# Rotary embedding on one core: when cosine is asked for, and how the last batch leaves

## The chip, the core and the metric

The kernel runs on one core of a Trainium2 chip. Its engines work side by side, each through its own list of instructions in order: VectorE (DVE) does the arithmetic, ScalarE (ACT) converts number formats, and GpSimd (POOL), SyncE (SP) and ACT issue DMA transfers. Tensors lie in the device memory; the engines work on the on-chip memory of 128 partitions. All transfers are carried by the same 16 DMA engines, fed from three queues: q0, the software queue, with what POOL issues; q1 with what SP issues; q10 with what ACT issues. [...] TensorE is not used.

The metric is device time in microseconds (us), the median over runs. Lower is better.

## The reference

`x` is float32 of shape (8, 2048, 16, 64): batch, position, head, head dimension. `cos` and `sin` are float32 of shape (2048, 32).

```python
x1 = x[..., :head_dim // 2]
x2 = x[..., head_dim // 2:]
out1 = x1 * cos - x2 * sin      # cos, sin broadcast over batch and head
out2 = x1 * sin + x2 * cos
return np.concatenate([out1, out2], axis=-1).astype(np.float32)
```

It reads 67 MB and writes 67 MB, with three vector operations for each element.

## The kernel before

**Tiling.** Each of the 128 partitions holds 16 neighbouring positions, called rows here (J = 16; a row is H x D = 1024 numbers, 4 KB in float32). A batch is 16 rows per partition. `buf` has five float16 slots of one batch each; batch b lies in slot b mod 5.

**Tables.** `sin_f` and `cos_f` come in as float32 by SP (line 50) and ACT (line 51). ACT makes float16 copies: `sin_h` with the negated sine in its first half (lines 101 and 102), `cos_h` (line 103).

**Rotation.** `rotate(b, j0, j1)` has three DVE operations: `v` = swapped halves times `sin_h` (line 87), `x` times `cos_h` in place (line 91), and their sum in place (line 93).

**The software queue.** All of POOL's transfers go through `queue` (line 57), which keeps them in program order. Loads and stores of whole batches and pairs of batches go there: load rows 2 to 15 of batch 0; store row 0 of batch 0; load batches 1 and 2; load 3 and 4; store rows 1 to 15 of batch 0; store 1 and 2; load 5; load 6 and 7; store 3 and 4; store 5 and 6; and the last rows of batch 7. POOL waits at each for what it needs, so a transfer is issued only when the one before it has been issued.

**The start.** The first two rows of batch 0 do not go through the software queue. ACT asks for them, as float32, into `head`, which is a view of the still unused last slot (line 52). ACT then narrows them to float16 into slot 0 in two steps, `narrow_head(0, 1)` and `narrow_head(1, 2)` (line 96). In ACT's order this stands behind the cosine copy of line 103. After the first step DVE rotates row 0, POOL stores it, and behind that store POOL issues the loads of batches 1 to 4.

**The end.** Batch 7 leaves in three pieces: rows 0 to 8 and rows 9 to 13 as two software stores, and rows 14 and 15 as float32: ACT widens them into `tail`, a view of slot 3 (line 127), and SP stores them (line 128). A dependency added by hand (`gate`) holds SP's store back until the store of rows 0 to 8 has landed.

Of the kernel before, what the change touches and what calls it, by code (L numbers as in the profile page):

```python
# [1 line left out]

# [4 lines left out]


@with_exitstack  # L10
def kernel(
    ctx: ExitStack,
    tc: tile.TileContext,
    x: bass.AP,
    cos: bass.AP,
    sin: bass.AP,
    out: bass.AP,
):
    nc = tc.nc
    f16 = mybir.dt.float16  # L20
    f32 = mybir.dt.float32

    B, S, H, D = x.shape
    Dh = D // 2
    P = nc.NUM_PARTITIONS
    J = S // P
    SLOTS = 5
    JA = 2
    JE = 2
    JF = 1  # L30

    pool = ctx.enter_context(tc.tile_pool(name="rope", bufs=1))
    buf = pool.tile([P, SLOTS, J, H, D], f16)
    v = pool.tile([P, J, H, D], f16)
    sin_f = pool.tile([P, J, Dh], f32)
    cos_f = pool.tile([P, J, Dh], f32)
    cos_h = pool.tile([P, J, Dh], f16)
    sin_h = pool.tile([P, J, D], f16)

    def words(slot, rows):  # L40
        flat = buf[:, slot, 0 : 2 * rows].rearrange("p j h d -> p (j h d)")
        return flat.bitcast(f32)

    head = words(SLOTS - 1, JA)
    tail = words(SLOTS - 2, JE)
    rows_in = x.rearrange("b (p j) h d -> p b (j h d)", j=J)
    rows_out = out.rearrange("b (p j) h d -> p b (j h d)", j=J)
    W = H * D

    nc.sync.dma_start(out=sin_f, in_=sin.rearrange("(p j) d -> p j d", j=J))  # L50
    nc.scalar.dma_start(out=cos_f, in_=cos.rearrange("(p j) d -> p j d", j=J))  # L51
    nc.scalar.dma_start(out=head, in_=rows_in[:, 0, 0 : JA * W])

    ring = []

    def queue(dst, src):
        dma = nc.gpsimd.dma_start(out=dst, in_=src)  # L57
        if ring:
            tc.add_manual_dep(
                dma.ins,  # L60
                ring[-1].ins.name,
                mybir.DependencyInfo(mybir.DependencyClass.NoSync, mybir.DependencyReason.DATA),
                reason="order of the ring",
            )
        ring.append(dma)
        return dma

    def part(b, n, j0, j1):
        s = b % SLOTS
        return buf[:, s : s + n, j0:j1].rearrange("p n j h d -> p n (j h d)")  # L70

    def load(b, n=1, j0=0):
        return queue(part(b, n, j0, J), rows_in[:, b : b + n, j0 * W : J * W])

    def store(b, n=1, j0=0, j1=J):
        return queue(rows_out[:, b : b + n, j0 * W : j1 * W], part(b, n, j0, j1))

    def rotate(b, j0=0, j1=J):
        n = j1 - j0
        js = slice(j0, j1)  # L80
        xt = buf[:, b % SLOTS, js]
        vt = v[:, js]
        shape = [P, n, H, 2, Dh]
        sin_b = sin_h[:, js, :].rearrange("p j (e d) -> p j e d", e=2).unsqueeze(2).to_broadcast(shape)
        cos_b = cos_h[:, js, :].unsqueeze(2).to_broadcast([P, n, 2 * H, Dh])
        xe = xt.rearrange("p j h (e d) -> p j h e d", e=2)
        nc.vector.tensor_mul(  # L87
            out=vt.rearrange("p j h (e d) -> p j h e d", e=2), in0=xe[:, :, :, ::-1, :], in1=sin_b
        )
        xw = xt.rearrange("p j h (e d) -> p j (h e) d", d=Dh)  # L90
        nc.vector.tensor_mul(out=xw, in0=xw, in1=cos_b)  # L91
        xa = xt.rearrange("p j h d -> p (j h d)")
        nc.vector.tensor_add(out=xa, in0=xa, in1=vt.rearrange("p j h d -> p (j h d)"))  # L93

    def narrow_head(j0, j1):
        nc.scalar.copy(  # L96
            out=buf[:, 0, j0:j1].rearrange("p j h d -> p (j h d)"), in_=head[:, j0 * W : j1 * W]
        )

    load(0, j0=JA)  # L100
    nc.scalar.copy(out=sin_h[:, :, Dh:D], in_=sin_f)  # L101
    nc.scalar.mul(out=sin_h[:, :, 0:Dh], in_=sin_f, mul=-1.0)  # L102
    nc.scalar.copy(out=cos_h, in_=cos_f)  # L103
    narrow_head(0, JF)
    narrow_head(JF, JA)
    rotate(0, 0, JF)
    store(0, j1=JF)
    load(1, 2)
    load(3, 2)
    rotate(0, JF, J)  # L110
    store(0, j0=JF)
    rotate(1)
    rotate(2)
    store(1, 2)
    load(5)
    load(6, 2)
    rotate(3)
    rotate(4)
    store(3, 2)
    rotate(5)  # L120
    rotate(6)
    store(5, 2)
    rotate(7)
    gate = store(7, j1=9)
    store(7, j0=9, j1=J - JE)

    nc.scalar.copy(out=tail, in_=buf[:, (B - 1) % SLOTS, J - JE : J].rearrange("p j h d -> p (j h d)"))  # L127
    end = nc.sync.dma_start(out=rows_out[:, B - 1, (J - JE) * W : J * W], in_=tail)
    tc.add_manual_dep(
        end.ins,  # L130
        gate.ins.name,
        mybir.DependencyInfo(mybir.DependencyClass.Sync, mybir.DependencyReason.DATA),
        reason="the last rows go out behind this part",
    )


# [1 line left out]
_INS = ['x', 'cos', 'sin']  # L138
_OUTS = [((8, 2048, 16, 64), 'float32')]


# [23 lines left out]
```

## Time and profile before

| What | Value |
| --- | --- |
| median of 3 runs | 316.48 us (316.36 to 316.49) |
| the profiled execution's own time | 316.32 us |
| its span | 314.6 us |
| DVE busy | 209.1 us, 66% |
| ACT busy | 6.8 us, 2% |
| POOL busy | 7.9 us, 3% |
| moved by DMA | 101.71 MB; 67.63 MB read from and 67.11 MB written to the device memory |
| one DVE operation on a batch | 8.69 us, 7 times in each of three lines |
| store of rows 0 to 8 of batch 7 | 4608 KB, 35.5 us from issue to landing |
| store of rows 9 to 13 of batch 7 | 2560 KB, 41.0 us |
| SP's store of rows 14 and 15 | 1024 KB, issued at 305.26, 8.4 us |
| the transfers of ACT and SP at the start | head 1024 KB, 12.1 us; cosine 256 KB, 3.9 us; sine 256 KB, 3.7 us |

The span is the profiled part of an execution; 1.72 us of the execution's own time lie around it. Sizes of loads are those of the data that arrive, so a software load that converts to float16 counts half of what it reads. In the rows of the profile "a<-b" names what is written and read, an engine name with q (ACTq, SPq) is that engine's sequencer issuing a transfer, and the part in brackets tells how long the engine had been idle and what ended the wait. In lists of stretches each line has the stretch, its length, busy time and number of instructions of DVE, ACT and POOL, the TensorE clock (of no meaning here), the mean share of the 16 DMA engines and GB/s. A packet is counted in the stretch in which it ends, so a share can be over 1.

### The profile page before, as it was taken

The page shows a single profiled execution, that of the slowest core. Times are in us where ns is not written, and L with a number is a line of the kernel's source. Part 1 is how long each engine was busy: PE and PEld are TensorE (multiplying, and loading weights), DVE is VectorE, ACT ScalarE, POOL GpSimd, SP SyncE. Part 2 cuts the span into 40 slices and gives each one's busy share as a digit, 9 for nine tenths or more (in the row PEclk, how much of TensorE's full clock was granted, in tenths as well). Part 3 has the DMA queues.
Part 4 walks back from the last instruction along what each step waited for, and adds up shares of the span by engine and source line. Part 5 has one row for each costly group of instructions (what it writes and reads, how often), then busy time and mean ns, then how long its engine had stood idle before and what let it go on. Part 6 is the DMA issues. An engine that isn't in the chain of part 4 may idle for free.

```text
span 314.6 us, 113 instructions
## 1 busy us (share of the span) xinstructions
DVE 209.1 (66%) x27; ACT 6.8 (2%) x7; POOL 7.9 (3%) x16
## 2 busy tenths in 40 slices
DVE  0109991089999999999994399903999999200000
ACT  3200000000000000000000000000000000200000
POOL 1020000000000000000000000000000000100000
DMA  7989999999999899999999999999999999999998
GB/s 230 261 193 249 267 200 200 200 267 200 200 200 325 375 500 400 400 400 533 400 200 221 246 200 200 250 217 333 400 517 417 400 400 525 408 400 400 433 425 342
DMA packets 3072, 101.71 MB, mean 323 GB/s; under 512 B 256, under 2 KB 256, under 8 KB 640
## 3 DMA queue, kind: packets, MB, share of 16 engines
q0 software_dynamic: 2496, 99.09, 98.1%
q1 hardware_dynamic: 288, 1.31, 1.2%
q10 hardware_dynamic: 288, 1.31, 1.0%
HBM read 67.63 MB, written 67.11 MB: 428 GB/s over the span
## 4 chain that ended last, share of the span: by engine, by line
DVE 59%; DMA 19%; another core or an unknown queue 7%; ACT 1%; issue 0%; POOL 0%; ACTq 0%; DVEq 0%
DVE v L87 20%; DVE buf L91 20%; DVE buf L93 20%; DMA buf<-in_x_dram 19%; ACT buf L127 1%; ACT buf L96 0%; POOL out_dram L57 0%; ACTq L51 0%; DVEq L87 0%
## 5 line engine op out<-in xcount | busy, mean ns | idle before, releaser
L87 DVE TENSOR_TENSOR v<-buf,sin_h 128x16384 f16<-128x16384 f16 (+2 forms) x9 | 69.7, 7744 | 59.7 <-DMA buf<-in_x_dram 45.3
L91 DVE TENSOR_TENSOR buf<-buf,cos_h 128x16384 f16<-128x16384 f16 (+2 forms) x9 | 69.7, 7744 | 0.3
L93 DVE TENSOR_TENSOR buf<-buf,v 128x16384 f16<-128x16384 f16 (+2 forms) x9 | 69.7, 7744 | 0.3
L57 POOL DMA_DIRECT2D out_dram<-buf x7 | 4.3, 620 | 219.7 <-DVE buf L93 219.7
L127 ACT CAST buf<-buf 128x2048 f32<-128x2048 f16 x1 | 1.9, 1897 | 254.2 <-DVE buf L93 254.2
L57 POOL DMA_DIRECT2D buf<-in_x_dram x5 | 3.4, 679 | 43.0 <-DMA out_dram<-buf 42.2
L96 ACT CAST buf<-buf 128x1024 f16<-128x1024 f32 x2 | 2.0, 1042 | 7.2 <-DMA buf<-in_x_dram 7.2
L101 ACT ACT_TABLE_LOAD x1 | 1.3, 1283 | 1.7 <-PEq L149 1.7
L101 ACT CAST sin_h<-sin_f 128x512 f16<-128x512 f32 x1 | 0.6, 617 | 1.5 <-DMA sin_f<-in_sin_dram 1.5
L102 ACT ACTIVATE sin_h<-sin_f 128x512 f16<-128x512 f32 x1 | 0.6, 624 | 0.0
L103 ACT CAST cos_h<-cos_f 128x512 f16<-128x512 f32 x1 | 0.6, 601 | 0.0
L149 POOL MEMSET const-float32-0.0<- 128x1 f32 x1 | 0.1, 99 | 0.2 <-issue 0.2
L149 POOL MEMSET const-bfloat16-1.0<- 128x1 bf16 x1 | 0.1, 102 | 0.0
L149 POOL MEMSET const-float32-1.0<- 128x1 f32 x1 | 0.1, 99 | 0.0
L149 POOL MEMSET const-uint8-127<- 128x1 uint8 x1 | 0.1, 99 | 0.0
## 6 DMA issues: line engine op xcount, KB each, us to landing
buf<-in_x_dram POOLq DMA_DIRECT2D x3, 8192.0 KB, 57.1
out_dram<-buf POOLq DMA_DIRECT2D x1, 7680.0 KB, 71.7
out_dram<-buf POOLq DMA_DIRECT2D x1, 4608.0 KB, 35.5
buf<-in_x_dram POOLq DMA_DIRECT2D x1, 4096.0 KB, 57.3
buf<-in_x_dram POOLq DMA_DIRECT2D x1, 3584.0 KB, 22.6
out_dram<-buf POOLq DMA_DIRECT2D x1, 2560.0 KB, 41.0
buf<-in_x_dram ACTq DMA_DIRECT2D x1, 1024.0 KB, 12.1
out_dram<-buf SPq DMA_DIRECT2D x1, 1024.0 KB, 8.4
```

Source lines behind the costliest of these rows:

```text
L57: dma = nc.gpsimd.dma_start(out=dst, in_=src)
L87: nc.vector.tensor_mul(out=vt.rearrange("p j h (e d) -> p j h e d", e=2), in0=xe[:, :, :, ::-1, :], in1=sin_b)
L91: nc.vector.tensor_mul(out=xw, in0=xw, in1=cos_b)
L93: nc.vector.tensor_add(out=xa, in0=xa, in1=vt.rearrange("p j h d -> p (j h d)"))
L96: nc.scalar.copy(out=buf[:, 0, j0:j1].rearrange("p j h d -> p (j h d)"), in_=head[:, j0 * W : j1 * W])
L101: nc.scalar.copy(out=sin_h[:, :, Dh:D], in_=sin_f)
L102: nc.scalar.mul(out=sin_h[:, :, 0:Dh], in_=sin_f, mul=-1.0)
L103: nc.scalar.copy(out=cos_h, in_=cos_f)
L127: nc.scalar.copy(out=tail, in_=buf[:, (B - 1) % SLOTS, J - JE : J].rearrange("p j h d -> p (j h d)"))
L149: nc = _bacc.Bacc("TRN2", target_bir_lowering=False, num_devices=1)
```

## The change

At the start, SP asks for `head` behind sine, in place of ACT. ACT then asks for cosine alone. Ahead of it ACT copies one word per partition, from a word that DVE has set to zero; the first such operation on ACT makes it load its table, which before was loaded at line 101. A dependency added by hand makes the cosine request wait for the copy to end. In the built program ACT's list therefore begins with the table load, the copy, the request for cosine (with a wait on ACT's own semaphore), and goes on with lines 101 to 103 and 96 of the old file as before.

At the end, the two software stores of batch 7 become one of 14 rows, and SP's store of the last two rows is held back until the store of batches 5 and 6 has landed, instead of rows 0 to 8 of batch 7. POOL's list has one transfer less. All else is the same.

```diff
     nc.sync.dma_start(out=sin_f, in_=sin.rearrange("(p j) d -> p j d", j=J))
-    nc.scalar.dma_start(out=cos_f, in_=cos.rearrange("(p j) d -> p j d", j=J))
-    nc.scalar.dma_start(out=head, in_=rows_in[:, 0, 0 : JA * W])
+    nc.sync.dma_start(out=head, in_=rows_in[:, 0, 0 : JA * W])
+    word = pool.tile([P, 2], f32)
+    nc.vector.memset(word[:, 0:1], 0.0)
+    warm = nc.scalar.copy(out=word[:, 1:2], in_=word[:, 0:1])
+    cosine = nc.scalar.dma_start(out=cos_f, in_=cos.rearrange("(p j) d -> p j d", j=J))
+    tc.add_manual_dep(
+        cosine.ins,
+        warm.ins.name,
+        mybir.DependencyInfo(mybir.DependencyClass.Sync, mybir.DependencyReason.DATA),
+        reason="the first rows are asked for ahead of cosine",
+    )
...
     rotate(6)
-    store(5, 2)
+    gate = store(5, 2)
     rotate(7)
-    gate = store(7, j1=9)
-    store(7, j0=9, j1=J - JE)
+    store(7, j1=J - JE)
```

## The prediction

> **What bounds the kernel now.** I read the page's DMA rows first, then the chain of waits and the timeline of the first 26 us, then the stretches and DMA queues of the start, then those of the last 12 us.
>
> ```profile
> DMA  7989999999999899999999999999999999999998
> q0 software_dynamic: 2496, 99.09, 98.1%
> DVE 59%; DMA 19%; another core or an unknown queue 7%; ACT 1%; issue 0%; POOL 0%; ACTq 0%; DVEq 0%
> ```
>
> The chain names DVE for 59%, but DVE works for 66% of the span and waits 59.7 us ahead of L87, while the 16 DMA engines are busy in every slice and the software queue alone takes 98.1%. In the finely cut stretches full-batch load or store rows follow one another every 2.4 us from 24.6 to 291.3 us, with no hole. So DMA is the bound: a hole in its stream is added to the end, and work elsewhere costs nothing until it makes one. The change can make a hole in one place, the start.
>
> ```profile
> 0.73 0.39 ACTq L51 DMA_DIRECT2D cos_f<-in_cos_dram  x1
> 0.74 0.38 SPq L50 DMA_DIRECT2D sin_f<-in_sin_dram  x1
> 1.15 0.47 ACTq L52 DMA_DIRECT2D buf<-in_x_dram  x1
> 1.25 0.67 POOL L57 DMA_DIRECT2D buf<-in_x_dram  x1 [0.80 <-PEq L160]
> 1.65 1.28 ACT L101 ACT_TABLE_LOAD   x1 [1.65 <-PEq L149]
> 5.51 0.60 ACT L103 CAST cos_h<-cos_f 128x512 f16<-128x512 f32 x1
> 13.26 1.99 ACT L96 CAST buf<-buf 128x1024 f16<-128x1024 f32 x2 [7.15 <-DMA buf<-in_x_dram]
> 16.79 0.53 POOL L57 DMA_DIRECT2D out_dram<-buf  x1 [14.88 <-DVE buf L93]
> 17.31 1.43 POOL L57 DMA_DIRECT2D buf<-in_x_dram  x2
> ```
>
> Times are start and length. Three small transfers are asked for before the 14-row load of batch 0 (POOL, 1.25). Head ends ACT's wait at 13.26; 3.5 us later POOL stores row 0, and only behind that store are the loads of batches 1 to 4 issued (17.31). Until then the software queue holds nothing but the 14-row load. Next, stretches of the start: duration, busy times, clock, DMA share, GB/s.
>
> ```profile
> 6.00:7.75 1.75, 0.00 (x0) 0.11 (x1) 0.00 (x0) 1.00 0.00 0
> 7.75:8.50 0.75, 0.00 (x0) 0.00 (x0) 0.00 (x0) 1.00 3.27 786
> 8.50:10.25 1.75, 0.00 (x0) 0.00 (x0) 0.00 (x0) 1.00 0.00 0
> 10.25:11.00 0.75, 0.00 (x0) 0.00 (x0) 0.00 (x0) 1.00 3.27 786
> 21.00:21.50 0.50, 0.00 (x0) 0.00 (x0) 0.00 (x0) 1.00 4.27 918
> 21.50:23.00 1.50, 0.00 (x0) 0.00 (x0) 0.00 (x0) 1.00 0.00 0
> 23.00:24.50 1.50, 0.56 (x1) 0.00 (x0) 0.00 (x0) 1.00 1.01 341
> ```
>
> A packet counts where it ends, so a zero stretch is no idle DMA but one long row under way in each engine. Rows of the 14-row load end every 2.1 us, the eighth and last of each engine at 21.0 to 21.5; the store of row 0 follows from 23.0. What travels with them is read from the queues, cut to 2.5:5.5, then 7.75:8.5, then 12.5:13:
>
> ```profile
> q10 hardware_dynamic: 235, 1.01, 82.6%
> ...
> q0 software_dynamic: 16, 0.46, 283.9%
> q10 hardware_dynamic: 16, 0.13, 42.9%
> ...
> q10 hardware_dynamic: 16, 0.00, 4.4%
> ```
>
> In the first stretch ACT's queue moves cosine (128 packets, 16 completion words) and 91 head rows; six head rows per engine are over by 6.0, before a second load row. After that each load row of an engine lets **one** packet of the other queue pass: head's seventh at 7.75 to 8.5, its eighth at 10.25 to 11, its completion word at 12.5 to 13. Hence 12.1 us for head.
>
> **The change part by part.**
>
> *Head on SP's queue.* It is issued behind sine, 0.74 + 0.38 + 0.03 = 1.15, as now. SP has nothing else until the tail. Instead of cosine, sine is ahead of it, also 256 KB. Bounds for its landing: now (13.24), or some 4 us sooner if cosine's 8 packets no longer share. Worth nothing: the limit below comes later.
>
> *Table load, word, copy.* The two ACT issues (0.73 to 1.62) no longer precede the table load, so it runs 0.73 to 2.01. The memset on DVE has no row; the four POOL memsets of 128x1 take 0.10 each, DVE is idle until 14.34: nothing. The copy of one word: casts of 512, 1024 and 2048 elements take 0.61, 1.04 and 1.90, which leaves 0.19 at zero elements. Cosine is issued at about 0.73 + 1.28 + 0.19 + 0.1 = 2.3 instead of 0.73, and the issue is over at 2.7. Queued behind it on ACT: the sine casts, waiting for sine until 4.45 anyway, so those lose nothing; then the cosine cast, and **behind that the narrowing of head**, since ACT works in order.
>
> *Where cosine lands.* Sine's first packets end in the slice from 1.75, 1.0 after its issue; cosine's now in the slice from 2.5, 1.8 after. So cosine's new first packets are ready at 3.3 to 4.1. The first load rows, 2.13 us each (425.8% of a half microsecond for 16 packets on 16 engines), end in 5.5 to 6.0, so they began at 3.4 to 3.9. Cosine thus meets a software queue that is already flowing. Its 8 packets and completion word then go one per load row, as head's last ones did; with none ahead of the first load row the ninth comes when the eight load rows are through: between 21.25 and 23.3, where the next thing now flows. I take 22.3, and ACT goes on 0.3 later: Y = 22.6 (21.5 to 23.7 as bounds).
>
> *What is late next.* After Y: cosine cast (the next ACT instruction starts 0.53 to 0.60 later), then the present chain from head's landing to the row store, 16.79 - 13.24 = 3.55. POOL issues the store at Y + 4.1 and the load 0.5 later. From a software issue to its first packet end: at least sine's 1.0 (a hardware queue), at most 4.5 (the first load, 1.25 to about 5.75, which had six head rows of 0.32 = 1.9 us in its way). The latter is the same queue, so 4.5 - 1.9 = 2.6. The first packet of the row store comes at Y + 6.7, where it now comes at 23.3: a hole of Y - 16.6 = **6.0 us**. The loads come 0.5 behind the store, whose 0.52 MB take 1.2 us, so they add none. DMA has no slack later, and DVE and POOL work follows from loads and stores that all shift alike: the 6.0 us reach the end. If cosine landed before 16.6, the cover would be whole and the cost nothing.
>
> *The end.* One POOL issue less (0.5 us, at 270, hidden behind 24 us of queued stores). The two parts land at 269.72 + 35.5 = 305.2 and 270.3 + 41.0 = 311.3; 2.62 MB in 6.1 us against 6.0 at the 437 GB/s of the full rows (1.05 MB in 2.4 us): splitting costs 0.1. Tail's gate moves from 305.2 to about 294.4 (243.55 + 50.8), so its 8 packets per engine can pass between the 14-row ones, and the software store may end last. Bytes are the same. Tail alone now moves 1.05 MB in some 2.6 us, 0.2 over that rate. A software store is seen landed 0.5 after its completion words (304.75 to 305.2), tail 0.4 after (313.25 to 313.66). So -0.3 to +0.3; I take 0.
>
> [...]
>
> **Sum.** Profiled execution 316.32 (314.6 span, 1.72 around it) + 6.0 + 0 = **322.3**; the median, 316.48, is 0.16 above that execution, which is within rounding here.
>
> **The rivals.**
>
> 1. *Not slower: cosine gets through ahead of the load rows.* Unhindered, it would land 3.9 after its issue as now, at 6.2, far before 16.6; the hole is nil: 316.5. For it: six head rows got through by 6.0, four of them while the first load row was recorded as under way, and cosine's packets are a quarter of head's. It decides if at least five of cosine's nine packets are ahead of the first load row; the completion word then goes with the fifth load row or before, at about 15. Against it: tail, issued at 305.26, moved nothing until 310.5, when all eight rows of the five-row store were out; a late small transfer waited for what was queued. [...] 22%.
>
> 2. *Half way: some of cosine's packets slip ahead.* With two to four of the nine ahead, the completion word goes with load row eight to six (21.2 to 17.0), Y is 21.6 to 17.4, the hole 5.0 to 0.8; middle 319. The start times (3.3 to 4.1 against 3.4 to 3.9) allow it. 16%.
>
> 3. *Faster: the last completion was exposed and is saved.* From the last rows of the five-row store (310.0) to its landing (311.3) are 1.3 us; if rival 1 holds at the start, and that is what merging removes, 315.0 to 315.8. Against it, tail's packets fill that time (1.05 MB from 310.5 on). 7%.
>
> **How the numbers follow.** The forecast has 55%: 322.3. Its own range takes Y from 21.5 to 23.7 and the issue delay from 1.0 to 4.5: hole 21.5 + 4.1 + 1.0 - 23.3 = 3.3 to 9.0, so 319.6 to 325.3. The range of all, 316.2 to 324.6, takes in rivals 1 and 2 and leaves out rival 3, a sliver of rival 1 and the longest delays, some 16%. What can be told from no change is 0.2%, 0.63 us. Slower: 55 + 16 = 71%. Same: 22%. Faster: 7%.
>
> **What would show it.** In the profile after: cosine's issue on ACT near 2.3 and its landing some 20 us later; the cosine cast at 21.5 to 24 with ACT idle before it, released by cosine's DMA; head landed well before; POOL's row store near 26.7 instead of 16.79; no DMA traffic from about 23 to 29, a low digit in the third or fourth slice; the load of batches 1 and 2 landing near 70 instead of 63.7; all later spacings as now, and the last landings within 0.3 us of today's distance from the store of batches 5 and 6. I am wrong if the cosine cast runs before 16, if the row store is issued late but DMA has no hole, or if the end gains a microsecond.

## The result and the profile after

The changed kernel takes 323.69 us (median of 5 runs, 323.47 to 323.89) against 316.42 us before (5 runs, 316.36 to 316.49): ratio 1.0231, 95% interval 1.0216 to 1.0245, 7.27 us longer. Its profiled execution took 323.65 us, its span 321.9 us; before, 316.32 and 314.6. The spans differ by 7.3 us, so the traces account for the whole of it.

The start in the timeline after (start, length, instruction, idle time before it and what ended it):

```profile
0.73 1.28 ACT L54 ACT_TABLE_LOAD   x1 [0.73 <-PEq L157]
1.25 0.68 POOL L66 DMA_DIRECT2D buf<-in_x_dram  x1 [0.81 <-PEq L168]
2.25 0.36 ACTq L55 DMA_DIRECT2D cos_f<-in_cos_dram  x1
23.78 0.62 ACT L112 CAST cos_h<-cos_f 128x512 f16<-128x512 f32 x1 [19.05 <-DMA cos_f<-in_cos_dram]
27.83 0.53 POOL L66 DMA_DIRECT2D out_dram<-buf  x1 [25.89 <-DVE buf L102]
28.35 1.43 POOL L66 DMA_DIRECT2D buf<-in_x_dram  x2
```

Cosine is asked for at 2.25 instead of 0.73, and ACT gets it at 23.78, having waited 19.05 us. Head had landed at 1.17 + 9.1 = 10.3 and lay there. The row store goes out at 27.83 instead of 16.79, and the loads of batches 1 to 4 behind it.

Stretches of DMA after, in the columns named before (stretch, length, DVE, ACT, POOL, clock, DMA share, GB/s):

```profile
20.50:21.25 0.75, 0.00 (x0) 0.00 (x0) 0.00 (x0) 1.00 2.97 655
21.25:22.75 1.50, 0.00 (x0) 0.00 (x0) 0.00 (x0) 1.00 0.00 0
22.75:23.50 0.75, 0.00 (x0) 0.00 (x0) 0.00 (x0) 1.00 0.15 44
23.50:28.75 5.25, 3.31 (x4) 2.51 (x3) 0.92 (x2) 1.00 0.00 0
28.75:30.25 1.50, 1.50 (x1) 0.00 (x0) 1.03 (x2) 1.00 1.16 371
```

One thing about these lists was read wrongly ahead of the result: a packet is counted in the stretch in which it starts, not in the one in which it ends. A load row is one packet of the software queue, what one engine moves for one partition; in the first load it is 14 rows of `x`, 28 KB on arrival (16 packets are 0.46 MB). Finer cuts of the profile before show head's seventh rows, then load rows, then head's eighth rows:

```profile
7.80:8.10 0.30, 0.00 (x0) 0.00 (x0) 0.00 (x0) 1.00 1.07 437
8.10:8.40 0.30, 0.00 (x0) 0.00 (x0) 0.00 (x0) 1.00 7.10 1529
...
10.20:10.50 0.30, 0.00 (x0) 0.00 (x0) 0.00 (x0) 1.00 1.07 437
```

Each of the three holds 16 packets, one for each engine, so length times share is the time of one: 0.32 us for a head row, 2.13 us for a load row. The load rows are recorded 0.3 us behind the head rows, and the next head rows 2.1 us behind the load rows. What lies between two records is thus the length of the earlier packet, so the records are starts. In the profile before, the first load rows then start at 5.7 to 6.0.

The eighth load row of each engine starts at 20.5 to 21.25 (before: 21.0 to 21.5) and is over 2.13 us later. At 22.75 to 23.5 there are only last packets of cosine and completion words (so called here: one packet under 512 B of each engine behind its part of a transfer, 32 in this stretch), and then nothing for 5.25 us, with no long row under way any more. Before, the row store's packets followed from 23.0. That is the hole. What travelled at the start and beside the load rows after, the queues cut to 3.5:5.2, then 5.2:5.75, then 14:14.5 and then 22.75:23.5 (packets, MB, share):

```profile
q1 hardware_dynamic: 90, 0.74, 102.2%
...
q0 software_dynamic: 16, 0.46, 387.1%
...
q0 software_dynamic: 16, 0.46, 425.8%
q10 hardware_dynamic: 16, 0.03, 19.2%
...
q10 hardware_dynamic: 32, 0.03, 14.0%
q0 software_dynamic: 16, 0.00, 1.2%
```

Up to 5.2 the engines move head's rows (q1) and nothing of cosine, though it was asked for at 2.25; then come the first load rows, and cosine's first packets only behind these. With each load row of 16 engines go 16 packets of cosine, one for each engine, and so from the second load row to the eighth. The last 32 (the eighth packet and the completion word of each engine) come when the load rows are through.

The end, from the list of transfers after:

```profile
out_dram<-buf POOLq DMA_DIRECT2D x1, 7168.0 KB, 43.0
out_dram<-buf SPq DMA_DIRECT2D x1, 1024.0 KB, 19.3
```

The 14-row store, issued at 277.04, lands at 320.0; tail, issued at 301.70, at 321.0. The last full-batch row starts in a burst centred on 298.7 after and 291.3 before, so from there to the end of the span it is 23.2 us after and 23.3 before. Nothing was won or lost at the end.

### The profile page after: what moved, and what is told of

Read it like the earlier page. It is cut to its first block, busy times and chain, and to the rows that moved or that the text cites. A ratio compares the mean times of both kernels' runs of the same rounds, so it can differ in the third digit from the quotient of the medians.

```text
span 321.9 us, 114 instructions
## 1 busy us (share of the span) xinstructions
DVE 209.1 (65%) x28; ACT 7.0 (2%) x8; POOL 7.3 (2%) x15
## 4 chain that ended last, share of the span: by engine, by line
DVE 57%; DMA 20%; another core or an unknown queue 7%; ACT 2%; issue 0%; POOL 0%; DVEq 0%
DVE v L96 19%; DVE buf L100 19%; DVE buf L102 19%; DMA buf<-in_x_dram 13%; DMA cos_f<-in_cos_dram 7%; ACT buf L135 1%; ACT L54 0%; ACT buf L105 0%; ACT cos_h L112 0%; POOL out_dram L66 0%; ACT word L54 0%; DVEq L96 0%
```

## The experiments

Each kernel is compared with before as run beside it on the same chip; before took 316.35 to 316.44 in these groups.

### The end alone, and the start alone

`e1_end_only`: the start of before, the end of the change.

```diff
-    store(5, 2)
+    gate = store(5, 2)
     rotate(7)
-    gate = store(7, j1=9)
-    store(7, j0=9, j1=J - JE)
+    store(7, j1=J - JE)
```

> Only the end of the change: one store of fourteen rows, tail behind the store of batches 5 and 6; the start is that of before. My theory (the whole loss is made at the start): within 0.3 us of before, 316.1 to 316.8, and the last landing as far from the last full-batch row as in before (23.3 us from that row to the end of the span). Rival (the merge moves the end): 1 us or more to either side, 315.4 or 317.4.

Measured 316.47 (11 runs) against 316.43: ratio 1.0001, interval 0.9992 to 1.0010.

`e2_front_only`: the changed kernel with the end of before.

```diff
-    gate = store(5, 2)
+    store(5, 2)
     rotate(7)
-    store(7, j1=J - JE)
+    gate = store(7, j1=9)
+    store(7, j0=9, j1=J - JE)
```

> Only the start of the change: head on SP, cosine asked for behind the table load and the copy; the end is that of before. My theory: 323.4 to 324.0, the same as the whole change, with the cosine cast near 23.8 and no DMA packet from about 23.5 to 28.8. Rival (part of the 7.3 us is from the merged end): 323.0 or less.

Measured 323.86 (4 runs), ratio 1.0237, interval 1.0223 to 1.0251; the cosine cast ran at 23.82. The whole loss is made at the start, and merging the stores is worth nothing that can be measured. One DMA less gave 0.0 us; it lay in a queue whose packets take 98.1% of the engines' time in the profile before.

### Is it the queue or the lateness?

`e3_no_wait`: head goes by SP and the end is merged, but cosine is asked for at once.

```diff
     nc.sync.dma_start(out=head, in_=rows_in[:, 0, 0 : JA * W])
-    word = pool.tile([P, 2], f32)
...
-    cosine = nc.scalar.dma_start(out=cos_f, in_=cos.rearrange("(p j) d -> p j d", j=J))
-    tc.add_manual_dep(
...
+    nc.scalar.dma_start(out=cos_f, in_=cos.rearrange("(p j) d -> p j d", j=J))
```

> Head is on SP's queue behind sine and the end is merged, as in the change, but cosine is asked for by ACT at once, without the copy and the wait. My theory (it is the lateness of the request, not the move of head): cosine lands near 4.6, head before 13.3, no hole, 316.0 to 316.8. Rival (head behind sine on one queue, or cosine alone on its queue beside load rows, is enough to delay the start): cosine lands at 10 or later, or the time is above 318.

Measured 316.49 (11 runs), ratio 1.0002, interval 0.9993 to 1.0011. Cosine is issued at 0.74 and lands 3.6 us later; the narrowing of head starts at 13.07. Moving head to SP's queue costs nothing; the late request does.

### Is it the hole that costs?

`e4_loads_first`: the change, with two lines in the other order.

```diff
-    store(0, j1=JF)
     load(1, 2)
+    store(0, j1=JF)
     load(3, 2)
```

> The change, but the load of batches 1 and 2 stands ahead of the store of row 0 in the software queue. Cosine is as late as in the change. My theory (lateness costs only because the software queue runs dry): cosine cast still near 24, DMA without a hole, 316.2 to 317.2. Rival (the late rotation costs by itself, through DVE or a later wait): 320 or more.

Measured 316.46 (11 runs, 316.26 to 317.35), ratio 1.0004, interval 0.9996 to 1.0013. A line of its timeline and one of its stretches:

```profile
23.84 0.62 ACT L112 CAST cos_h<-cos_f 128x512 f16<-128x512 f32 x1 [19.27 <-DMA cos_f<-in_cos_dram]
```

```profile
22.75:23.50 0.75, 0.00 (x0) 0.00 (x0) 0.00 (x0) 1.00 3.39 743
```

Cosine, asked for at 2.25, is as late, and the whole rotation of batch 0 with it. But at 22.75 to 23.5, where the change has 44 GB/s of leftovers, the first rows of batch 1 start, and the time is that of before. The late transfer cost nothing by itself here (ratio 1.0004); what cost the 7.3 us of the change is that the software queue held nothing behind the first load.

### Does cosine move one packet per load row?

`e5_split_load`: the change, with the first software load cut into two of seven rows, which makes each load row half as long.

```diff
-    load(0, j0=JA)
+    queue(part(0, 1, JA, 9), rows_in[:, 0:1, JA * W : 9 * W])
+    load(0, j0=9)
```

> The change, but rows 2 to 15 of batch 0 are asked for as two loads of seven rows, so that a load row of an engine is 28 KB of the input and takes about 1.05 us instead of 2.1. Cosine is asked for as late as in the change. My theory (cosine moves one packet per load row): its packets still go one per load row, but the ninth comes after nine short rows, at 14 to 16.5; the row store then starts before the load rows are through, no hole, 316.2 to 317.0. Rival (cosine has to wait until the first rows are all in): cosine cast near 23.8 and 323.0 to 324.0.

Measured 316.55 (10 runs), ratio 1.0003, interval 0.9993 to 1.0013. Its cosine cast:

```profile
15.71 0.62 ACT L113 CAST cos_h<-cos_f 128x512 f16<-128x512 f32 x1 [11.05 <-DMA cos_f<-in_cos_dram]
```

Asked for at 2.25 as in the change, cosine lands 8 us sooner, since the rows that it takes turns with are half as long (1.08 us against 2.13); the row store is issued at 19.75, before the load rows are through, and there is no hole. As in the change, 16 of cosine's packets went with the 16 load rows of each burst from the second (6.25 to 7) to the eighth (13.5 to 14.25), and the last 32 beside the ninth (14.5 to 15.25): one passed per load row.

### From which request on is it too late?

`e6_delay_256`, `e6_delay_640` and `e6_delay_1024`: in place of ACT's copy, a DVE memset of that many words stands ahead of cosine's request.

```diff
-    word = pool.tile([P, 2], f32)
-    nc.vector.memset(word[:, 0:1], 0.0)
-    warm = nc.scalar.copy(out=word[:, 1:2], in_=word[:, 0:1])
+    word = pool.tile([P, 640], f32)
+    warm = nc.vector.memset(word, 0.0)
```

> The change, but instead of ACT's table load and copy a DVE memset of 256 words per partition stands ahead of cosine's request, so that it is made at about 1.1 to 1.2. My theory (packets that are ready before the first load row pass freely, the others go one per load row): all or nearly all of cosine's packets are ahead, it lands by 8, 316.2 to 316.8. Rival (any request behind the software load is too late): lands at 20 or later, above 321.

> As the kernel with 256 words, with 640 words: request at about 1.5 to 1.6. My theory: some packets are ahead; landing between 6 and 22, always beside a load row (steps of 2.2 us); the time is that of before if it lands before 18, and 1 us or more longer if it lands after 20. Rival (a threshold of another kind): either lands by 6 or at 23.8 with nothing between in all three kernels.

> As the kernel with 256 words, with 1024 words: request at about 1.9 to 2.1. My theory: few packets or none are ahead; landing 17 to 23.8, time 316.4 to 323.9 by the same rule, the row store's first packet 5.1 us behind the landing and the hole counted from 23.3. Rival: as above.

| Kernel | cosine asked for | cosine cast at | time, us | runs |
| --- | --- | --- | --- | --- |
| 256 words | 1.17 | 5.90 | 316.39 (316.21 to 323.72) | 10 |
| 640 words | 1.56 | 23.75 | 323.80 (323.66 to 325.51) | 4 |
| 1024 words | 1.97 | 23.71 | 323.74 | 4 |
| the change | 2.25 | 23.78 | 323.69 | 5 |

POOL asks for the software load at 1.25 in all of them. A request 0.08 us before it is early, one 0.3 us behind it is as late as one 1.0 us behind. I had expected steps in between and there were none: a step between 1.17 and 1.56, as the rival had it. With 256 words 142 of cosine's 144 packets start between 2.75 and 5.25, among head's rows. With 640 words none starts before 5.2; then 15 engines start one just ahead of their first load row, so at most one of nine is ahead. Head is asked for at 1.15 to 1.17 in all of them, so the late requests stand 0.4 us and more behind head's as well as 0.3 us and more behind the load's; these three kernels can't tell which of the two matters. Nine of the ten runs with 256 words took 316.21 to 316.62 and one 323.72, which looks like the same race lost once; no trace of that run was taken.

### By the clock, or by the software load?

`e8_load_waits`: the change, and POOL's first load waits for ACT's copy as well.

```diff
-    load(0, j0=JA)
+    first = load(0, j0=JA)
+    tc.add_manual_dep(
+        first.ins,
+        warm.ins.name,
+        mybir.DependencyInfo(mybir.DependencyClass.Sync, mybir.DependencyReason.DATA),
+        reason="the first software load behind the copy too",
+    )
```

> The change, but POOL's load of rows 2 to 15 of batch 0 waits for ACT's copy too, so it is asked for at about 2.3, together with cosine, instead of 1.25. My theory (what counts is whether cosine is asked for before or after the software load, not the time by the clock): cosine lands by 8 although it is asked for as late as in the change, and the time is 316.2 to 317.6 (up to 1 us for the later first load). Rival (a request at 2.25 is too late by the clock): cosine cast at 20 or later, 322 or more.

Measured 321.90 (4 runs, 319.75 to 322.35; ratio 1.0162, interval 1.0128 to 1.0197); the cosine cast ran at 22.44. That is the rival's landing and all but its time, but the queues tell why. Cut to 5:6.5, all packets of 5.99:6.41, and 10:11.25:

```profile
q10 hardware_dynamic: 128, 0.24, 47.6%
...
DMA packets 59, 0.47 MB, mean 1112 GB/s; under 512 B 13, under 2 KB 13, under 8 KB 45
...
q10 hardware_dynamic: 3, 0.00, 1.1%
```

Of cosine's 144 packets 128 are through by 6.5, 13 completion words among them, so 13 of the 16 engines are done (in the second line the 13 packets under 512 B). The other 16 packets belong to three engines (one engine has only nine in all) and go beside the load rows: three with the second rows, three with the third, two with each of the next. That fits one engine that is two packets behind and two that are seven behind, each passing one per load row. The transfer landed only when the last of them was done, so three engines that took a load row first delayed cosine by about 16 us. The expectation of the next kernel speaks of one engine; it was three. In that kernel the load stands well behind cosine.

`e9_load_later`: as that kernel, but the load waits for three DVE memsets.

```diff
+    slow = pool.tile([P, 1024], f32)
+    nc.vector.memset(slow, 0.0)
+    nc.vector.memset(slow, 0.0)
+    late = nc.vector.memset(slow[:, 0:512], 0.0)
...
-    load(0, j0=JA)
+    first = load(0, j0=JA)
+    tc.add_manual_dep(
+        first.ins,
+        late.ins.name,
...
```

> The change, but POOL's load of rows 2 to 15 of batch 0 waits for three DVE memsets and is asked for at about 3.3, 1 us behind cosine (0.27 behind it in the kernel where the load waited for the copy, where one DMA engine of 16 still let its load rows go first and cosine was landed at 22.4). My theory (cosine is late on every engine whose load rows are ready first, and lands with its last engine): now no engine has a load row ready before cosine, cosine lands by 8, the row store is issued by 17, and the time is 316.4 to 318.4, that is before plus what the first load is late. Rival (cosine is late for another reason, whatever the load does): cosine cast at 20 or later, 321 or more.

```profile
2.25 0.36 ACTq L59 DMA_DIRECT2D cos_f<-in_cos_dram  x1
4.12 0.68 POOL L70 DMA_DIRECT2D buf<-in_x_dram  x1 [3.68 <-DVE slow L58]
6.67 0.62 ACT L122 CAST cos_h<-cos_f 128x512 f16<-128x512 f32 x1 [1.99 <-DMA cos_f<-in_cos_dram]
```

The memsets took longer than planned and the load was asked for at 4.12. Cosine, asked for as late as in the change, lands 4.4 us later, the row store goes out at 10.72, and the time is 318.10 (10 runs, 316.77 to 320.01; ratio 1.0050, interval 1.0028 to 1.0073). The time by the clock is thus not what decides, but which an engine starts first, cosine's packets or its first load row. In both kernels cosine's packets start only after 5.0, when head's rows are nearly all through; here the load rows start behind them (from 5.9), in the change they start at 5.2 to 5.75. So a late cosine comes first behind head's rows, and by then the load rows are there. Why it does not pass among head's rows stays open; a late request without head ahead of it was not run. This kernel's times spread over 3 us; in its trace (319.40) one engine starts its first load row at 7.8, the others at 5.9 to 6.3, and one is still on a load row at 102.7 when the others have gone on to the store. The other runs were not traced.

### The second slip

In the change the rows lie 5.7 us behind those of before at the row store, 6.45 us behind from the second load row on, and 7.35 us behind from the first store row after the loads of batches 1 to 4 on. That last step, the last load rows and the first store rows, after and then before:

```profile
105.50:106.25 0.75, 0.75 (x1) 0.00 (x0) 0.00 (x0) 1.00 4.37 699
109.00:109.50 0.50, 0.50 (x1) 0.00 (x0) 0.00 (x0) 1.00 4.60 1966
```

```profile
99.25:99.75 0.50, 0.50 (x1) 0.00 (x0) 0.00 (x0) 1.00 4.86 1049
101.75:102.25 0.50, 0.50 (x1) 0.00 (x0) 0.00 (x0) 1.00 4.60 1966
```

Since records are starts, no wait lies between: the last load row itself took longer, 4.37 x 0.75 = 3.28 us on the mean against 4.86 x 0.50 = 2.43. The step before it, at the first load rows behind the hole, looks the same: they took 2.96 us on the mean (3.72 x 0.80, less a few completion words) and the second ones 2.43.

```profile
30.20:31.00 0.80, 0.80 (x1) 0.00 (x0) 0.00 (x0) 1.00 3.72 655
33.00:34.00 1.00, 1.00 (x1) 0.00 (x0) 0.00 (x0) 1.00 2.43 524
```

`e7_hole_order` (the change) and `e7_plain_order` (start of before, merged end) both move one load:

```diff
-    load(3, 2)
     rotate(0, JF, J)
     store(0, j0=JF)
+    load(3, 2)
```

> The change, but the load of batches 3 and 4 stands behind the store of rows 1 to 15 in the software queue. Asked: in every kernel with the hole the rows slip another 0.85 us at the first switch from load rows to store rows, some 76 us after the hole, and in none without it. Theory A (the slip belongs to the first such switch after a restart): it now comes near 70, where load rows of batch 2 give way to the store, and the total stays 323.2 to 324.0. Theory B (it belongs to the place near 106 or to the load of batches 3 and 4): no step at 70, total 322.6 to 323.2 or a step elsewhere.

> The same order of the software queue without the hole: start as in before, merged end. Both theories: 316.2 to 316.9 and no step at the first switch from load rows to store rows, near 64. If the step is there too, it has nothing to do with the hole.

Measured 324.00 (4 runs) with the hole and 316.37 (10 runs; ratio 1.0000, interval 0.9990 to 1.0009) without. With the hole the step moved along: the last load row of batch 2, from 67 on, took 3.36 us on the mean, and 2.43 without the hole, from 60.75 on. So with a hole the slip lies at the first switch from load rows to store rows after it, at both places tried. It is not wholly bound to the hole: `e4_loads_first`, which has none, shows a smaller one at its first switch (3.68 x 0.75 = 2.76 us at 59.0 to 59.75). What makes it is not settled.

## Why the prediction was right, point by point

The forecast was 322.3, a hole at the start and nothing at the end; what bounds the kernel, one packet per load row and the hole were as forecast. Four sizes in the sum were off by amounts that partly cancel (+1.2, -1.6, +0.8, +0.85), and one step, that cosine meets load rows already under way, came out right by luck. That the time came within 1.4 us is in part luck too.

| Step of the sum | forecast | measured |
| --- | --- | --- |
| cosine asked for | 2.3 | 2.25 |
| ACT goes on with cosine (Y) | 22.6 (21.5 to 23.7) | 23.78 |
| from there to the row store's issue | 4.1 | 27.83 - 23.78 = 4.05 |
| from that issue to the start of its first packets | 2.6 (1.0 to 4.5) | about 1.0 (27.83 to the stretch from 28.75) |
| loads behind the row store | 0 | about 0.8 |
| slack or cost later | 0 | about 0.85 |
| the end | 0 (-0.3 to 0.3) | -0.1; alone 0.0 |

- **What bounds it: right.** The hole reached the end in full, though DVE has the larger share of the chain (57% against 20% for DMA); the kernel without the hole but with all the late work took 316.46.
- **"Cosine thus meets a software queue that is already flowing": right in the outcome, by luck.** I took the first load rows to begin at 3.4 to 3.9 and cosine's first packets to be ready at 3.3 to 4.1. The first was a record read as an end: the load rows began at 5.7 to 6.0 before, and at 5.2 to 5.75 after. With that and cosine ready at 4.1, its eight packets (about 0.1 us each, 19.2% of half a microsecond for 16) would have been through ahead of the load rows, which is rival 1. What held cosine back was something that the prediction lacked: it did not pass among head's rows, which took until after 5.2. The head rows "recorded" beside the first load row, in rival 1, ran ahead of it.
- **Cosine one packet per load row: right**, shown by the rows after and by the halved rows. It landed 1.2 us later than my middle, just outside the bounds, because the eighth load rows were not over at 21.5 but ran on to about 23, and the last two of cosine's nine packets start only then.
- **The delay of a software store: mis-sized by 1.6 us.** I took the first load's 4.5 us less the six head rows that were in its way, 2.6. The low end, from sine, was the true one: with idle engines the first packets started about 1.0 after the issue. In the kernel whose load was asked for at 4.12 its first rows start 1.8 later, right behind cosine. Why the load that is asked for at 1.25 starts only after 5.2 is not explained by the six rows.
- **"So they add none", of the loads: wrong by 0.8 us.** The second load row came that much later than the row store had been. About 0.5 of it is the first load row, which took 2.96 us instead of 2.43; the rest is a later start of that row. Why is open.
- **"DMA has no slack later" and all shift alike: right as to slack**, but one more slip of 0.85 us came at the next switch from loads to stores.
- **The end: right**, 316.47 for the end alone.
- **Rival 1 (cosine gets through)** did not happen in the change, but is what happens with a request at 1.17 or a later load. **Rival 2 (half way)** was badly weighed: across all engines no such case was seen; the nearest is three engines of 16 being behind, and that cost 5.55 us where all 16 cost 7.3. **Rival 3** fell with the end alone.

7.3 us is then 5.7 at the row store, which is the hole, 0.75 more at the first load rows, 0.9 at the switch to the store and -0.1 at the end; the bursts resolve no more than a tenth.

## What to carry to other kernels

Before delaying a small transfer, ask which queue with long rows will be flowing by then: here its packets passed one per load row of 2.13 us on each engine, and it landed with the slowest of them, so 256 KB took 21.5 us instead of 3.9. Where a queue's next transfers hang on such a landing, put work that needs nothing in between: swapping two lines took the 7.3 us away without touching the late request. Merging two stores at the end was worth nothing here (316.47 us against 316.43).

## What the runs showed of the hardware

- The edge was sharp: 0.39 us in the time of the request (1.17 to 1.56) moved the cosine cast by 18 us. On the early side cosine's packets passed among head's rows (142 of 144 from 2.75 to 5.25); on the late side none started before 5.1, when head's rows were nearly through.
- In one trace 3 of 16 engines lost the race alone, and the transfer was as late as the last of them: 128 of its 144 packets were through by 6.5, and it landed at 22.4.
- After the hole the stream slipped twice more, about 0.8 us at the first load rows and 0.85 us at the first switch from load to store rows. In both the load rows themselves took longer (2.96 and 3.28 us against 2.43). Of the kernels without a hole one had a smaller slip at its first switch (2.76 us), and the cause is open.
